# The gate and up products of two FFNs as seven half-size block products instead of eight

## The chip, the cores and the metric

The kernel runs on one core of one Trainium2 chip. The metric is the time of one execution on the device in microseconds; a kernel is run several times, and the median counts. The engines have the profile's names: PE is TensorE, which multiplies matrices (PEld its weight loads), DVE is VectorE, ACT ScalarE, POOL GpSimd, and SP's queue issues the DMA transfers.

## The reference

One decoder layer over T = 512 tokens with D = 1024 and FF = 2816, in float32:

```python
def swiglu(x, w_gate, w_up, w_down):
    return (jax.nn.silu(x @ w_gate) * (x @ w_up)) @ w_down
...
x = layer_norm(ALPHA * x + 0.5 * swiglu(x, ffn1_w_gate[l], ffn1_w_up[l], ffn1_w_down[l]), ln1_g[l], ln1_b[l])
proj = x @ w_in[l]
...
mix = jnp.concatenate([o_a, o_b], axis=-1) @ w_out[l]
x = layer_norm(ALPHA * x + mix, ln2_g[l], ln2_b[l])
x = layer_norm(ALPHA * x + 0.5 * swiglu(x, ffn2_w_gate[l], ffn2_w_up[l], ffn2_w_down[l]), ln3_g[l], ln3_b[l])
```

Between the two FFNs, `o_a` is a gated linear recurrence with four heads and `o_b` a depthwise convolution; this part is called the mixer here.

## The kernel before, in words

**Exact products in f32r.** Every operand of a large product is split into a high part (a cast to f32r on ScalarE) and a low part (the value less its high part, on VectorE): `split`, L59 to L61. `mm3` (L99 to L102) multiplies high by high, high by low and low by high into the same PSUM bank, so one product of 128x128 by 128x512 costs three matmuls.

**Weights.** They come in units of 128x1024 values. `fetch` (L64) issues the DMA on SP's queue, casts (`whi`, L60) and subtracts (`wlo`, L61). Six units' parts fit on chip (`SLOTS`), raw units have two buffers, and `ahead` keeps four units ready beyond the one in use.

**An FFN** (`ffn`, L243). The transposed activations x lie on chip as `xh`, `xl`. For each of 22 column blocks f of 128 columns there is a gate unit and an up unit: eight k of `mm3` each, 24 matmuls of 512 columns (the tokens). Then `evacuate` (L250 to L253): silu of the gate's bank on ScalarE, the product with the up bank on VectorE, and the cast and subtraction that make `hh`, `hl`, the parts of h. The first two column blocks are done differently: in FFN1 with the first four units and x arriving in growing pieces (L279 to L295), in FFN2 by `four_halved` (below).

**The down phase** is `rows_out` (L160): two halves of 512 output columns, 11 units each, four token tiles in four banks. The last four units of the second half go token tile by token tile. As each tile is done, VectorE adds it to the residual (L177) and takes statistics (L178, L182), GpSimd takes the root, VectorE scales (L186, L190), and TensorE transposes the normed tile (L134), whose parts ScalarE and VectorE make (L138). PE's order there is written by hand: tile 2's transposes, filler matmuls, tile 3's transposes and the rest of the filler. The filler, `four_halved` (L230), is the next phase's first four units over 256 columns, the first two token tiles before the others; before FFN2 these are its first two column blocks.

Outside the hand-written stretches a scheduler sets each engine's order when the program is built; on the chip an engine takes its instructions strictly in that order.

Of the kernel before, what the change touches and what calls it, by code (L numbers as in the profile page):

```python
# [16 lines left out]
P = 128  # L17
T = 512
# [4 lines left out]
NF = FF // P  # L23
NH = 4
# [21 lines left out]
def decoder_layer(ctx, tc, x_tok, x_t, vec, bcast, ng, w_gu1, w_d1, w_i, w_g, w_col, w_o, w_gu2, w_d2, out):  # L46
# [17 lines left out]
    def fetch(src, shape, lo_engine):  # L64
        raw = raws.tile([P, 1024], F32, tag="raw", name="raw")
        hi = parts.tile([P, 1024], F32R, tag="whi", name="whi")
        lo = parts.tile([P, 1024], F32R, tag="wlo", name="wlo")
        nc.sync.dma_start(out=raw, in_=src)
        split(raw, hi, lo, lo_engine)
        a, b = shape  # L70
        return hi.rearrange("p (a b) -> p a b", a=a), lo.rearrange("p (a b) -> p a b", a=a)

    todo, ready = deque(), deque()

    def ahead(n):
        while todo and len(ready) < n:
            ready.append(fetch(*todo.popleft()))

    def plan(srcs, shape, lo_engine):
        todo.extend((s, shape, lo_engine) for s in srcs)  # L80

    def unit():
        ahead(1 + AHEAD)
        return ready.popleft()

    tok, ch = (2, 512), (NK, P)
    plan([w_gu1[f, s] for f in range(2, NF) for s in range(2)], ch, nc.vector)
    plan([w_d1[h, u] for h in range(2) for u in range(NF // 2)], tok, nc.vector)
# [16 lines left out]
    xh = act.tile([P, NK, T], F32R, name="xh")  # L105
    xl = act.tile([P, NK, T], F32R, name="xl")
# [8 lines left out]
    gain = const.tile([P, D], F32, name="gain")  # L115
    bias = const.tile([P, D], F32, name="bias")

    def load_gb(i):
        nc.sync.dma_start(out=gain, in_=bcast[2 * i:2 * i + 1, :].broadcast_to([P, D]))
        nc.sync.dma_start(out=bias, in_=bcast[2 * i + 1:2 * i + 2, :].broadcast_to([P, D]))  # L120
# [18 lines left out]

    def scaled(i):  # L140
# [7 lines left out]
    def weave(main, fill):  # L148
        """main's steps, and as much of fill after each as its pause takes."""
# [10 lines left out]
    def rows_out(ks, per, lhs, accs, factor, late, finish, follow=()):  # L160
# [19 lines left out]
        def norm(i):  # L180
            mv = small.tile([P, 2], F32, tag="mv", name="mv")
# [12 lines left out]
        for u in range(n_units):  # L194
            hi, lo = unit()
            for i in range(NT):
                part(acc, u, hi, lo, i)
# [3 lines left out]
        for u in range(n_units - late):  # L201
            hi, lo = unit()
            for i in range(NT):
                part(acc, u, hi, lo, i)
        ahead(late)
        kept = [(u, *unit_now()) for u in range(n_units - late, n_units)]
        ahead(SLOTS - late)
        with tc.manual_schedule(engines={PE}):
            left = deque()
            for i in range(NT):  # L210
# [4 lines left out]
                if i == NT - 1:  # L215
# [11 lines left out]
    def unit_now():  # L227
        return ready.popleft()

    def four_halved(pp, banks):  # L230
        """Four units' columns, the first two token tiles before the others."""
        ahead(4)
        us = [unit_now() for _ in range(4)]
        pp.extend(bank(b) for b in banks)
# [8 lines left out]
    def ffn(first, meanwhile, finish, follow=()):  # L243
        with tc.tile_pool(name="ffn", bufs=1) as fp, tc.tile_pool(name="ffn2", bufs=2) as fp2:
            hh = fp.tile([P, NF, T], F32R, name="hh")
            hl = fp.tile([P, NF, T], F32R, name="hl")

            def evacuate(f, pg, pu):
                s = fp2.tile([P, T], F32, tag="s", name="s")
                nc.scalar.activation(s, pg, AF.Silu)  # L250
                nc.vector.tensor_tensor(s, pu, s, op=ALU.mult)  # L251
                nc.scalar.copy(hh[:, f, :], s)  # L252
                nc.vector.tensor_tensor(hl[:, f, :], s, hh[:, f, :].bitcast(F32), op=ALU.subtract)  # L253

# [18 lines left out]
    with tc.tile_pool(name="first", bufs=1) as fst:  # L273
        # the activation table loads while nothing else is there
# [4 lines left out]
        # the first four units and x come in interleaved, in growing pieces  # L279
        us = [(fst.tile([P, NK, P], F32, tag=f"raw{i}", name="raw"),  # L280
               *(parts.tile([P, 1024], F32R, tag=t, name=t).rearrange("p (a b) -> p a b", a=NK) for t in ("whi", "wlo")))
              for i in range(4)]
        for ks in (slice(0, 1), slice(1, 2), slice(2, 4), slice(4, 8)):
            x_raw = fst.tile([P, ks.stop - ks.start, T], F32, tag=f"xr{ks.start}", name="xr")
# [392 lines left out]
```

## Time and profile before

| | us |
|---|---|
| median of 3 runs | 977.93 (976.66 to 978.47) |
| profiled execution, span | 976.3 |
| TensorE busy, 4608 matmuls | 957.7 |
| its weight loads | 804.2 |
| VectorE busy | 472.1 |
| ScalarE busy | 276.0 |

Busy time is the sum over the span of what an engine's instructions took; matmuls overlap, so their recorded durations are longer than the distance from one start to the next. Where a cost is read below, it is read from starts. An operation over 128 partitions and 1024 elements in each is called 1024 wide.

### The profile page before, as it was taken

To read this page: it belongs to the slowest core of one execution; us is meant where nothing else is said; L and a number is where in the kernel's file an instruction comes from. 1 tells how busy PE (TensorE), PEld (TensorE's weight loads), DVE (VectorE), ACT (ScalarE), POOL (GpSimd) and SP (SyncE) were. 2 spreads that over 40 slices of the span, in tenths; PEclk is the share of its full clock that TensorE was granted. 3 is DMA by queue.
4 is the path that set the end of the run, shared out by engine and by line. 5 is a ranking of instruction groups with operands and counts; after the bars stand their busy time and mean duration, and the time that the engine had idled before them with its cause. 6 is when DMAs were issued, how large, how long until landed. Compare 5 with 4: busy or idle time off the path is not lost.

```text
span 976.3 us, 11214 instructions
## 1 busy us (share of the span) xinstructions
PE 957.7 (98%) x4608; PEld 804.2 (82%) x4608; DVE 472.1 (48%) x610; ACT 276.0 (28%) x376; POOL 119.9 (12%) x107
## 2 busy tenths in 40 slices
PE   7999999999999999999999999999999999999996
PEld 6888888888888889887888888988888888888885
DVE  6533333333224265999897658533333333322417
ACT  5423232323121213213331722432222223221200
POOL 8100000000000026522352203000000000000002
PEclk9999999999999999999999999999999999999998
DMA  7732323232222214311130121422222232323202
GB/s 265 247 116 87 108 87 106 88 105 90 98 97 96 98 44 141 130 65 50 59 127 4 65 93 43 172 103 90 105 88 107 87 107 87 108 87 109 87 21 87
DMA packets 28676, 96.49 MB, mean 99 GB/s; under 512 B 3200, under 2 KB 4736, under 8 KB 28496
## 3 DMA queue, kind: packets, MB, share of 16 engines
q1 hardware_dynamic: 28512, 95.43, 28.1%
q8 instruction: 36, 0.59, 0.2%
q0 software_dynamic: 112, 0.34, 0.2%
q14 instruction: 16, 0.13, 0.0%
HBM read 93.66 MB, written 2.10 MB: 98 GB/s over the span
## 4 chain that ended last, share of the span: by engine, by line
PE 81%; DVE 10%; issue 4%; POOL 2%; ACT 1%; DMA 1%; POOLq 0%; DVEq 0%; ACTq 0%
PE bank L101 26%; PE bank L102 26%; PE bank L100 26%; DVE bank L444 4%; PE bank L461 2%; DVE qk L493 1%; DVE xres L190 1%; POOL rstd L125 1%; DVE fq L411 1%; DVE diag L501 1%; POOL wlo L61 0%; DMA raw<-w_gu 0%; DVE tot L497 0%; DVE xl L138 0%; DMA raw<-w_g 0%
## 5 line engine op out<-in xcount | busy, mean ns | idle before, releaser
L100 PE MATMUL bank<-xh,whi 128*128 128x512 f32 (+1 forms) x896 | 336.9, 377 | 5.3 <-ACT whi L60 5.3
L101 PE MATMUL bank<-xl,whi 128*128 128x512 f32 (+1 forms) x896 | 335.8, 375 | 0.5 <-DVE xl L138 0.5
L102 PE MATMUL bank<-xh,wlo 128*128 128x512 f32 (+1 forms) x896 | 335.8, 375 | 0.0
L60 ACT CAST whi<-raw 128x1024 fp32r<-128x1024 f32 (+3 forms) x176 | 174.3, 995 | 560.2 <-PE bank L101 348.4
L61 DVE TENSOR_TENSOR wlo<-raw,whi 128x1024 fp32r<-128x1024 f32 (+3 forms) x154 | 176.8, 1155 | 301.1 <-ACT whi L60 297.1
L100 PEld LDWEIGHTS bank<-xh,whi 128*128 128x128 f32 x896 | 169.5, 189 | 35.7 <-ACT whi L60 5.8
L101 PEld LDWEIGHTS bank<-xl,whi 128*128 128x128 f32 x896 | 169.3, 189 | 30.7 <-DVE xl L138 0.8
L102 PEld LDWEIGHTS bank<-xh,wlo 128*128 128x128 f32 x896 | 169.3, 189 | 30.0
L100 PE MATMUL bank<-whi,hh 128*128 128x512 f32 x352 | 137.2, 390 | 0.0
L102 PE MATMUL bank<-whi,hl 128*128 128x512 f32 x352 | 137.0, 389 | 0.0
L101 PE MATMUL bank<-wlo,hh 128*128 128x512 f32 x352 | 137.0, 389 | 0.0
L124 POOL TENSOR_SCALAR rstd<-mv 128x1 f32<-128x1 f32 x16 | 8.1, 506 | 724.1 <-DVE mv L182 708.9
L251 DVE TENSOR_TENSOR s<-bank,s 128x512 f32<-128x512 f32 x44 | 30.3, 691 | 135.0 <-PE bank L102 134.3
L444 DVE SCALAR_TENSOR_TENSOR bank<-u,vecs,bank 128x512 f32<-128x512 f32 x120 | 82.0, 746 | 0.2
L102 PEld LDWEIGHTS bank<-whi,hl 128*128 128x128 f32 x352 | 66.1, 188 | 13.7
L100 PEld LDWEIGHTS bank<-whi,hh 128*128 128x128 f32 x352 | 66.1, 188 | 13.7
L101 PEld LDWEIGHTS bank<-wlo,hh 128*128 128x128 f32 x352 | 66.1, 188 | 13.5
L61 POOL TENSOR_TENSOR wlo<-raw,whi 128x1024 fp32r<-128x1024 f32 x22 | 53.0, 2414 | 78.3 <-ACT whi L60 78.2
L461 PEld LDWEIGHTS bank<-qk 128*128 128x128 f32 x256 | 30.6, 192 | 5.5 <-DVE qk L493 2.9
L461 PE MATMUL bank<-qk 128*128 128x128 f32 x256 | 31.8, 277 | 2.2 <-DVE qk L493 1.2
L253 DVE TENSOR_TENSOR hl<-s,hh 128x512 fp32r<-128x512 f32 x44 | 30.9, 703 | 0.0
L252 ACT CAST hh<-s 128x512 fp32r<-128x512 f32 x44 | 27.2, 622 | 0.0
(114 smaller groups left out, 601.5 us busy)
## 6 DMA issues: line engine op xcount, KB each, us to landing
raw<-w_gu SPq DMA_DIRECT2D x84, 512.0 KB, 3.2
raw<-w_d SPq DMA_DIRECT2D x44, 512.0 KB, 3.2
raw<-w_col SPq DMA_DIRECT2D x16, 512.0 KB, 3.2
raw<-w_o SPq DMA_DIRECT2D x8, 512.0 KB, 3.2
xres<-x_tok SPq DMA_DIRECT2D x4, 512.0 KB, 7.2
raw<-w_i SPq DMA_DIRECT2D x4, 512.0 KB, 3.1
raw<-w_g SPq DMA_DIRECT2D x4, 512.0 KB, 3.3
out<-xres SPq DMA_DIRECT2D x8, 256.0 KB, 2.0
```

What stands on the lines that cost most here:

```text
L60: nc.scalar.copy(hi, raw)
L61: lo_engine.tensor_tensor(lo, raw, hi.bitcast(F32), op=ALU.subtract)
L100: nc.tensor.matmul(ps, lhsT=lh, rhs=rh, start=first, stop=False)
L101: nc.tensor.matmul(ps, lhsT=lh, rhs=rl, start=False, stop=False)
L102: nc.tensor.matmul(ps, lhsT=ll, rhs=rh, start=False, stop=last)
L125: nc.gpsimd.tensor_tensor(r, r, negh.broadcast_to([P, n]) if n > 1 else negh, op=ALU.pow)
L190: nc.vector.scalar_tensor_tensor(xres[i][:, s], xres[i][:, s], r, bias[:, s], op0=ALU.mult, op1=ALU.add)
L251: nc.vector.tensor_tensor(s, pu, s, op=ALU.mult)
L252: nc.scalar.copy(hh[:, f, :], s)
L253: nc.vector.tensor_tensor(hl[:, f, :], s, hh[:, f, :].bitcast(F32), op=ALU.subtract)
L444: nc.vector.scalar_tensor_tensor(accs[n], us[n][:, j:j + T], vecs[:, w:w + 1], accs[n], op0=ALU.mult, op1=ALU.add)
L461: nc.tensor.matmul(ps[:, g, :], lhsT=k[:, h, sl], rhs=q[:, h, sl], start=True, stop=True)
```

## The change

**Seven products.** The tokens, the 1024 rows of a weight and the 2816 columns of a weight are each cut in half. A column block f of the first half of the columns goes together with block f + 11, so that there are 11 pairs of 2x2 block products. A gate block, and likewise an up block, is one `Quad`: a DMA of 1 MB with four 512-wide quarters b11, b12, b22, b21. With sums s1 to s4 of quarters of x and t1 to t4 of quarters of the weights, seven products p1 to p7 replace eight. Each is 4 k of three matmuls over 256 columns (half the tokens): 84 matmuls a block, where two units had 48 of 512 columns.

**The sums.** The x sums are made once per FFN (`Halves.sums`, four 1024-wide operations and the split of each). The weight sums are made for each block (`Quad.inner`): t1,t3 in one 1024-wide subtraction, t4 and t2 in two 512-wide ones. Every sum is split like a plain operand.

**The results.** A block has two PSUM banks, a and b. p2 is added onto p1, p4 onto p7 and p3 onto p5, each after ScalarE has copied the earlier one to SBUF (`Pair.steps`, L417); VectorE forms the sums (L419 to L422, L428). Silu and product are in `gate_up` (L473 to L477).

**h in f32.** h is no longer split at once but kept in f32, and the down phase's first half splits column pair u + 1 ahead of unit u (`before`, `parts_of`), into memory that held x and the early h. The gain and bias of each FFN's norm are loaded there too.

**The starts.** In FFN1, x comes in quarters and the first gate and up blocks in pieces; both p1 and both p2 go first (`EARLY`), the other products in the order of `LATER`. Before FFN2 the filler is these same four products (`begin`) and no longer four units; token tile 3's transposes are followed by `Halves.sums`.

```diff
@@ weights
+        def inner(self):
+            raw = self.raw
+            t13 = raws.tile([P, 2, 512], F32, tag="t13", name="t13", bufs=1)
+            nc.vector.tensor_tensor(t13, raw[:, 1:3, :], raw[:, 0:2, :], op=ALU.subtract)
+            self.both(("t1", "t3"), t13)
...
+            split(raw[:, 2:3, :], hi, lo, nc.vector)
+            self.name(("b22",), hi, lo)
+            nc.vector.tensor_tensor(raw[:, 1, :], raw[:, 2, :], t13[:, 0, :], op=ALU.subtract)
+            nc.vector.tensor_tensor(raw[:, 0, :], raw[:, 3, :], raw[:, 1, :], op=ALU.subtract)
+            self.both(("t4", "t2"), raw[:, 0:2, :])
@@ operand x
+        def sums(self):
+            (r11, r12), (r21, r22) = ([self.quarter(t, k) for k in range(2)] for t in range(2))
+            nc.vector.tensor_tensor(r22, r21, r22, op=ALU.add)
+            nc.vector.tensor_tensor(r21, r11, r21, op=ALU.subtract)
+            self.part("s3", r21)
+            self.part("s1", r22)
+            nc.vector.tensor_tensor(r11, r22, r11, op=ALU.subtract)
+            self.part("s2", r11)
+            nc.vector.tensor_tensor(r12, r12, r11, op=ALU.subtract)
+            self.part("s4", r12)
@@ products
+    SEVEN = {"p1": ("a11", "b11"), "p2": ("a12", "b21"), "p3": ("s4", "b22"), "p4": ("a22", "t4"),
+             "p5": ("s1", "t1"), "p6": ("s2", "t2"), "p7": ("s3", "t3")}
+    def product(ps, x, w, n, first=True):
+        xn, wn = SEVEN[n]
+        (xh, xl), (wh, wl) = x.of[xn], w[wn]
+        for k in range(4):
+            for j, (l, r) in enumerate(((wh, xh), (wh, xl), (wl, xh))):
+                nc.tensor.matmul(ps, lhsT=l[:, k, :], rhs=r[:, k, :], start=first and k == 0 and j == 0,
+                                 stop=k == 3 and j == 2, skip_group_check=True)
...
+                ps = {"p1": a[:, 0], "p2": a[:, 0], "p6": a[:, 1],
+                      "p7": b[:, 0], "p4": b[:, 0], "p5": b[:, 1], "p3": b[:, 1]}[n]
+                yield from product(ps, x, w, n, n in ("p1", "p5", "p6", "p7"))
+                if n in ("p1", "p7", "p5"):
+                    nc.scalar.copy(work[:, {"p1": 0, "p7": 1, "p5": 2}[n]], ps)
+                    if n == "p5":
+                        nc.vector.tensor_tensor(work[:, 1], work[:, 1], work[:, 2], op=ALU.add)
+                elif n == "p6":
+                    nc.vector.tensor_tensor(work[:, 0], a[:, 1], work[:, 0], op=ALU.add)
+                    nc.vector.tensor_tensor(work[:, 3], work[:, 0], work[:, 1], op=ALU.add)
...
+    EARLY, LATER = ("p1", "p2"), (("p7",), ("p4",), ("p5",), ("p6", "p3"))
+    USUAL = ("p1", "p7", "p2", "p4", "p5", "p6", "p3")
@@ ffn
-            for f in range(2, NF):
-                pp = []
-                for s in range(2):
-                    hi, lo = unit()
-                    ps = bank(2 * (f % 4) + s)
-                    for k in range(NK):
-                        mm3(ps, hi[:, k, :], lo[:, k, :], xh[:, k, :], xl[:, k, :], k == 0, k == NK - 1)
-                    pp.append(ps)
-                evacuate(f, *pp)
+                for f in range(1, NP):
+                    h.append(h_of(f))
+                    for s in range(2):
+                        ahead(3)
+                        w = unit_now()
+                        ahead(3)
+                        pr = Pair(pair_banks[f % 2][s], work_tile() if s else h[f])
+                        run(pr.steps(x, w, USUAL))
+                        gate_up(s, pr)
```

Three places show what this does to the engines' order.

VectorE, FFN1's start, before: behind the last piece of x come the last pieces of the first four units, and then the units after them.

```order
L61 TENSOR_TENSOR xl_74<-xr_153,xh_73 128x2048
L61 TENSOR_TENSOR wlo_95<-raw_93,whi_94 128x512
L61 TENSOR_TENSOR wlo_98<-raw_96,whi_97 128x512
L61 TENSOR_TENSOR wlo_101<-raw_99,whi_100 128x512
L61 TENSOR_TENSOR wlo_104<-raw_102,whi_103 128x512
L61 TENSOR_TENSOR wlo_271<-raw_269,whi_270 128x1024
L61 TENSOR_TENSOR wlo_277<-raw_275,whi_276 128x1024
```

The same place after the change; `xr_87` and `xr_88` are the raw quarters of x, `bl_86` holds the low parts of s1, s3 and s2 in this order, `raw_95` and `raw_96` are the first gate and up blocks, `t13_153` and `wlo_156` are the up block's t1,t3. Four operations stand between this piece and the split of a22 (`al_84`) ahead of it.

```order
L241 TENSOR_TENSOR xr_88<-xr_88 128x1024
L68 TENSOR_TENSOR wlo_128<-t13_125,whi_127 128x1024
L127 TENSOR_TENSOR raw_95<-raw_95 128x512
L242 TENSOR_TENSOR xr_88<-xr_87,xr_88 128x1024
L68 TENSOR_TENSOR bl_86<-xr_88,bh_85 128x1024
L68 TENSOR_TENSOR wlo_138<-raw_95,whi_137 128x1024
L68 TENSOR_TENSOR bl_86<-xr_88,bh_85 128x1024
L245 TENSOR_TENSOR xr_87<-xr_88,xr_87 128x1024
L120 TENSOR_TENSOR t13_153<-raw_96 128x1024
L247 TENSOR_TENSOR xr_87<-xr_87 128x1024
L68 TENSOR_TENSOR bl_86<-xr_87,bh_85 128x1024
L68 TENSOR_TENSOR wlo_156<-t13_153,whi_155 128x1024
```

The sums of x and both blocks' sums are now in one queue; the split of s3, which the first p7 needs, is the seventh row, and the last row is that of the up block's t3.

ScalarE, in the middle of FFN1's gate and up stage, before: each unit's cast, a silu, and the cast of h.

```order
L60 CAST whi_560<-raw_559 128x1024
L250 ACTIVATE s_554<-bank0_498 128x512
L60 CAST whi_591<-raw_590 128x1024
L252 CAST hh_324<-s_554 128x512
L60 CAST whi_627<-raw_626 128x1024
```

After the change, one gate block (`h_672` is its work tile, `bank4` its a, `bank6` its b) and the start of the up block (`work_1047`). The casts are those of a later block, `whi_1033` that of its t1,t3; the copies from `bank6` are those of p7 and p5.

```order
L417 COPY h_672<-bank4_930 128x256
L417 COPY h_672<-bank6_931 128x256
L65 CAST whi_1027<-raw_1025 128x1024
L65 CAST whi_1033<-t13_1031 128x1024
L417 COPY h_672<-bank6_931 128x256
L65 CAST whi_1043<-raw_1025 128x1024
L65 CAST w2hi_1037<-raw_1025 128x512
L417 COPY work_1047<-bank5_1048 128x256
L473 ACTIVATE h_672<-bank4_930 128x256
L474 ACTIVATE h_672<-h_672 128x768
L417 COPY work_1047<-bank7_1049 128x256
```

The cast of t1,t3 now stands ahead of the copy of p5, and the silu ahead of the up block's copy of p7.

VectorE, before FFN2, before the change: the last scaling of token tile 3 (`xres3_78`), the low parts of its transposes, and then units.

```order
L61 TENSOR_TENSOR wlo_4370<-raw_4368,whi_4369 128x1024
L190 SCALAR_TENSOR_TENSOR xres3_78<-xres3_78,rstd_4378,bias_86 128x512 x2
L138 TENSOR_TENSOR xl_74<-bank6_4479,xh_73 128x4x128
L138 TENSOR_TENSOR xl_74<-bank7_4486,xh_73 128x4x128
L61 TENSOR_TENSOR wlo_4613<-raw_4611,whi_4612 128x1024
L251 TENSOR_TENSOR s_4634<-bank1_4386,s_4634 128x512
```

After the change, from the same scaling on; `xr_5298` and `xr_5299` are raw quarters of x, `bl_5297` the low parts of s1 and s3, `raw_5301` and `raw_5625` weight blocks.

```order
L335 SCALAR_TENSOR_TENSOR xres3_76<-xres3_76,rstd_5481,m1_3845 128x512 x2
L68 TENSOR_TENSOR wlo_5612<-t13_5609,whi_5611 128x1024
L126 TENSOR_TENSOR raw_5301<-raw_5301,t13_5609 128x512
L278 TENSOR_TENSOR al_5295<-bank7_5565,ah_5294 128x4x128
L127 TENSOR_TENSOR raw_5301<-raw_5301 128x512
L120 TENSOR_TENSOR t13_5631<-raw_5625 128x1024
L241 TENSOR_TENSOR xr_5299<-xr_5299 128x1024
L68 TENSOR_TENSOR wlo_5622<-raw_5301,whi_5621 128x1024
L242 TENSOR_TENSOR xr_5299<-xr_5298,xr_5299 128x1024
L68 TENSOR_TENSOR bl_5297<-xr_5299,bh_5296 128x1024
L245 TENSOR_TENSOR xr_5298<-xr_5299,xr_5298 128x1024
L68 TENSOR_TENSOR bl_5297<-xr_5299,bh_5296 128x1024
```

Between the last transposes' low parts and the split of s3 now stand the sums of x and pieces of two weight blocks.

## Rows read from the trace of the kernel before

**Rows 1.** The page, part 1: engine, busy time, share of the span, instructions.
```profile
PE 957.7 (98%) x4608; PEld 804.2 (82%) x4608; DVE 472.1 (48%) x610; ACT 276.0 (28%) x376; POOL 119.9 (12%) x107
```

**Rows 2.** The page, part 4: the chain that ended last, shares of the span.
```profile
PE 81%; DVE 10%; issue 4%; POOL 2%; ACT 1%; DMA 1%; POOLq 0%; DVEq 0%; ACTq 0%
```

**Rows 3.** Windows: stretch, us; busy (count) of PE, PEld, DVE, ACT, POOL; PEclk, DMA, GB/s.
```profile
100.00:125.00 25.00, 25.00 (x112) 20.72 (x111) 8.71 (x9) 7.92 (x10) 0.00 (x0) 1.00 0.26 88
375.00:400.00 25.00, 25.00 (x191) 24.08 (x190) 14.85 (x22) 9.67 (x11) 16.52 (x9) 1.00 0.46 167
...
970.00:972.00 2.00, 0.00 (x0) 0.00 (x0) 1.56 (x3) 0.00 (x0) 1.68 (x2) 0.57 0.00 0
```

**Rows 4.** Timeline of VectorE, gate and up stage: start, duration, engine, line, operation, idle before.
```profile
106.53 0.69 DVE L251 TENSOR_TENSOR s<-bank,s 128x512 f32<-128x512 f32 x1 [3.42 <-PE bank L102]
...
117.41 0.69 DVE L251 TENSOR_TENSOR s<-bank,s 128x512 f32<-128x512 f32 x1 [3.42 <-PE bank L102]
```

**Rows 5.** Timeline of TensorE, 256-column fillers after FFN1's down phase.
```profile
374.77 0.28 PE L100 MATMUL bank<-xh,whi 128*128 128x256 f32 x1
...
379.69 0.28 PE L102 MATMUL bank<-xh,wlo 128*128 128x256 f32 x1
```

**Rows 6.** Timeline of TensorE: FFN1's first matmuls, and where each FFN's third column block begins.
```profile
6.71 0.63 PE L101 MATMUL bank<-xl,whi 128*128 128x512 f32 x1
7.13 0.63 PE L102 MATMUL bank<-xh,wlo 128*128 128x512 f32 x1
...
10.97 0.70 PE L100 MATMUL bank<-xh,whi 128*128 128x512 f32 x2
...
30.10 0.39 PE L100 MATMUL bank<-xh,whi 128*128 128x512 f32 x1
...
630.74 0.40 PE L100 MATMUL bank<-xh,whi 128*128 128x512 f32 x1
```

**Rows 7.** Timeline of VectorE: 1024-wide splits at the start, 512-wide ones before FFN2.
```profile
11.70 1.23 DVE L61 TENSOR_TENSOR xl<-xr,xh 128x1024 fp32r<-128x1024 f32 x1 [1.67 <-ACT xh L60]
12.84 1.95 DVE L61 TENSOR_TENSOR wlo<-raw,whi 128x256 fp32r<-128x256 f32 x4
...
604.33 1.27 DVE L138 TENSOR_TENSOR xl<-bank,xh 128x512 fp32r<-128x512 f32 x2
605.52 2.34 DVE L61 TENSOR_TENSOR wlo<-raw,whi 128x1024 fp32r<-128x1024 f32 x2
```

**Rows 8.** Timeline of ScalarE, at the start and in the gate and up stage.
```profile
5.66 0.21 ACT L307 ACTIVATE e<-e 128x8 f32<-128x8 f32 x1 [1.13 <-DVE e L306]
...
11.57 1.02 ACT L60 CAST whi<-raw 128x256 fp32r<-128x256 f32 x3
...
122.56 1.05 ACT L60 CAST whi<-raw 128x1024 fp32r<-128x1024 f32 x1 [3.80 <-PE bank L101]
123.51 0.59 ACT L250 ACTIVATE s<-bank 128x512 f32<-128x512 f32 x1
```

**Rows 9.** Timeline of both engines where a filler matmul waits for VectorE.
```profile
369.25 1.27 DVE L138 TENSOR_TENSOR xl<-bank,xh 128x512 fp32r<-128x512 f32 x2
...
369.98 0.38 PE L101 MATMUL bank<-xl,whi 128*128 128x256 f32 x1 [0.52 <-DVE xl L138]
370.20 0.28 PE L102 MATMUL bank<-xh,wlo 128*128 128x256 f32 x1
```

**Rows 10.** Timeline around the start of FFN2: VectorE's norms, TensorE's fillers and transposes.
```profile
599.17 0.67 DVE L177 SCALAR_TENSOR_TENSOR xres<-bank,xres 128x512 f32<-128x512 f32 x1
...
604.97 0.28 PE L100 MATMUL bank<-xh,whi 128*128 128x256 f32 x1
...
614.69 1.41 DVE L190 SCALAR_TENSOR_TENSOR xres<-xres,rstd,bias 128x512 f32<-128x512 f32 x2
...
615.58 1.29 PE L134 MATMUL bank<-ident,xres 128*128 128x128 f32 x8 [0.54 <-DVE xres L190]
```

**Rows 11.** The page, part 6: DMA issues, KB each, us to landing.
```profile
raw<-w_gu SPq DMA_DIRECT2D x84, 512.0 KB, 3.2
```

More of the change, by code (lines that the diff above doesn't have):

```diff
@@ L82, in unit, with plan_quads, plan_two, unit_now @@
+    def plan(srcs, shape, lo_engine):
+        todo.extend(("unit", s, shape, lo_engine) for s in srcs)
+    def plan_quads(srcs):
+        todo.extend(("quad", s) for s in srcs)
+    def plan_two(srcs):
+        todo.append(("two", *srcs))
+    def unit_now():
+        return ready.popleft()[1]
     def unit():
         ahead(1 + AHEAD)
-        return ready.popleft()
+        return unit_now()
     tok, ch = (2, 512), (NK, P)
-    plan([w_gu1[f, s] for f in range(2, NF) for s in range(2)], ch, nc.vector)
@@ L114, in decoder_layer, with load_gb @@
     masks = const.tile([P, len(MASKED) + 1, P], U8, name="masks")
[L115 to L120, printed above, removed]
+    gb = []
+    def load_gb(i, t):
+        gb[:] = [t[:, 0, :], t[:, 1, :]]
+        for j in range(2):
+            nc.sync.dma_start(out=t[:, j, :], in_=bcast[2 * i + j:2 * i + j + 1, :].broadcast_to([P, D]))
     def rstd_of(square, scale, eps, n):
@@ L158, in weave, with rows_out @@
                 owed -= t
-    def rows_out(ks, per, lhs, accs, factor, late, finish, follow=()):
+    def rows_out(ks, per, lhs, accs, factor, late, finish, follow=(), before=lambda u: None, then=lambda: None,
+                 fill=True):
         n_units = len(ks) // per
@@ L180, in norm @@
         def norm(i):
+            gain, bias = gb
             mv = small.tile([P, 2], F32, tag="mv", name="mv")
@@ L214, in rows_out @@
                         left.popleft()()
[L215 removed]
+                if i == NT - 1 and fill:
                     ahead(SLOTS)
@@ new lines, in decoder_layer, with work_tile, begin, early @@
+    EARLY, LATER = ("p1", "p2"), (("p7",), ("p4",), ("p5",), ("p6", "p3"))
+    USUAL = ("p1", "p7", "p2", "p4", "p5", "p6", "p3")
+    def work_tile():
+        return small.tile([P, 4, H], F32, tag="work", name="work", bufs=2)
+    def begin(begun, x, pair_banks):
+        ahead(2)
+        w2 = [unit_now() for _ in range(2)]
+        pairs = [Pair(pair_banks[0][s], work_tile()) for s in range(2)]
+        begun.extend((w2, pairs))
+        return early(x, w2, pairs)
+    def early(x, w2, pairs):
+        for n in EARLY:
+            for w, pr in zip(w2, pairs):
+                yield from pr.steps(x, w, (n,))
@@ L277, in decoder_layer, with load_x @@
         nc.scalar.activation(one, one, AF.Exp)
[L280 to L284, printed above, removed]
-            nc.sync.dma_start(out=x_raw, in_=x_t[:, ks, :])
-            for i, (raw, hi, lo) in enumerate(us):
-                nc.sync.dma_start(out=raw[:, ks, :],
-                                  in_=w_gu1[i // 2, i % 2, :, ks.start * P:ks.stop * P].rearrange("p (a b) -> p a b", b=P))
-            split(x_raw, xh[:, ks, :], xl[:, ks, :], nc.vector)
-            for raw, hi, lo in us:
-                split(raw[:, ks, :], hi[:, ks, :], lo[:, ks, :], nc.vector)
-        first = [bank(i) for i in range(4)]
-        for k in range(NK):
-            for ps, (_, hi, lo) in zip(first, us):
-                mm3(ps, hi[:, k, :], lo[:, k, :], xh[:, k, :], xl[:, k, :], k == 0, k == NK - 1)
-        ahead(2)
+        def load_x(t, k):
+            nc.sync.dma_start(out=x1.quarter(t, k), in_=x_q[t, k])
+        qs = [Quad(w_gu1[0, s]) for s in range(2)]
+        steps = [q.outer(True) for q in qs]
+        load_x(0, 0)
+        for q in qs:
+            q.load(0, 1)
+        load_x(0, 1)
+        for q in qs:
+            q.load(3, 4)
+        for k in range(2):
+            load_x(1, k)
+        for q in qs:
+            q.load(1, 3)
+        for k in range(2):
+            x1.part(f"a1{k + 1}", x1.quarter(0, k))
+            for st in steps:
+                st(k)
+        x1.part("a22", x1.quarter(1, 1))
+        qs[0].inner()
+        x1.sums()
+        qs[1].inner()
+        w2 = [q.of for q in qs]
+        pairs = [Pair(BANKS1[0][0][s], work_tile()) for s in range(2)]
+        with tc.manual_schedule(engines={PE}):
+            run(early(x1, w2, pairs))
         make_identity(nc, ident)
```

284 lines of the change are left out of this document (222 added, 62 removed).

## The prediction

> **What bounds the kernel now.** I read the page's busy shares first [rows 1]: TensorE is busy 98% of the 976.3 us, VectorE 48%, ScalarE 28%. The chain that ended last agrees [rows 2]: 81% TensorE, and only 4% in which an engine waited for nothing the profile shows. So time comes off by giving TensorE less to do, and goes on wherever TensorE is made to wait. The windows [rows 3] tell which stage has room: in the gate and up stage (100 to 125 us) TensorE is busy 25.00 of 25, VectorE 8.71, ScalarE 7.92. In 375 to 400, where matmuls are 256 columns wide, TensorE's own weight loads fill 24.08 of 25.
>
> The pitch comes from two timelines. VectorE multiplies a column block in at 106.53 and the next at 117.41 [rows 4]: 10.88 us for 48 matmuls of 512 columns, 0.2267 us each. The 256-column fillers start at 374.77 and, 41 matmuls later, at 379.69 [rows 5]: 0.120 us each. Two narrow ones cost 6% more than a wide one.
>
> **The steady blocks: −32.0.** One old unit pair (two units, 48 wide matmuls) is 10.88 us. One new block does the same work in 84 narrow ones, 84 × 0.120 = 10.08. Leaving out the first gate and up blocks of each FFN, that is 20 blocks a time: 20 × 0.80 = 16.0 for each FFN. The seven-for-eight saving alone would be 12.5%; the narrow pitch leaves 7.4%. The Trainium skill (TensorE: Matmul & The Clock Gate, section Back-to-back issue gap) lists 518 cycles for 512 columns and 262 for 256, so it would charge 1% for halving, not 6%; by it 48 wide ones less 84 narrow ones are 2856 cycles, 1.19 us at 2.4 GHz, a block, the term −47.6 and the time 965.9 (an estimate from that page). The trace does not agree, with 0.120 beside 0.2267; its rows are of this kernel's own f32r stream, and I use them.
>
> **VectorE under the steady blocks: nothing, narrowly.** Starts give the prices [rows 7]: a 1024-wide operation 12.84 − 11.70 = 1.14 us, a 512-wide one 0.60 (two in 605.52 − 604.33). A column block pair (a gate and an up block) needs eight 1024-wide, eight 512-wide, seven 256-wide and one 768-wide operation; with 0.34 and 0.87 estimated between and below those prices, 17.2 us of the 20.16 that TensorE takes. By the durations instead of the starts it is about 19.3. It fits if nothing stalls it; what it would cost without that cover is the second rival. ScalarE has four 1024-wide casts at 0.95 [rows 8] and smaller copies, 9.7 of 20.16. A block's 1 MB must come every 10 us where 0.5 MB came every 5.4 and landed in 3.2 us [rows 11]: hidden behind the blocks fetched ahead. In the down phase one more split of h (1.14 us) stands in each 5.4 us unit beside the unit's own 1.14: nothing, and the mixer's instructions stay. The gain and bias rows of each FFN's norm are now fetched on SP's queue between the units of the down phase's first half: nothing, since a transfer of that size (128x1024) lands in about 3.2 us [rows 11] and the norm is a half phase away.
>
> **Waits inside a block: +8.0.** Product p3 accumulates where p5 lay, so it waits for ScalarE's copy of p5. In ScalarE's order the cast of the next t1,t3 stands ahead of that copy, and it can only start when p5, the last reader of the old t1, is done. Behind the waiting p3 stand the next block's products, and VectorE's last sum waits for it. After p5: 0.08 us, cast 0.95, copy 0.38 (a 256-wide cast takes 0.31 [rows 8], a PSUM read a little more) = 1.41; then 0.05 to be seen (the first operation of the pair at 369.25 is done about 369.92, the matmul starts at 369.98 [rows 9]) and 0.10 for a matmul that waited (369.98 to 370.20 is 0.22 instead of 0.12) = 1.56 against the 1.44 of p6 that should cover it: 0.12 lost. In an up block the copy of p7 stands behind the silu, which waits for VectorE's last sum: about 0.05 more in half of the blocks. 40 blocks: 5.8, and about 1.1 in the first block of each FFN: 8.0. Bounds: 0, where the copy is in time by 0.1 us, and 16, where cast and copy each take 0.2 longer.
>
> **FFN1's start: +16.4.** Before, the first two column blocks are done at 30.10 [rows 6]. Now the operand sums go through VectorE first. ScalarE's first cast is queued behind the exponential at 5.66 [rows 8], so VectorE begins about 6.9 and is through the first six splits (two wide, four of 512: 4.7) at 11.6. Its next row needs the cast of a22, which ScalarE has queued behind the copies of both p1; these run at the slow pitch of 0.427 for 512 columns [rows 6], 0.22 for 256, and end at 13.2; copies and cast (0.95) take it to 14.8. From that row to the split of s3 (the second bl_86 in the order shown) stand eight wide operations and three of 512, 10.9: 25.7, and the first p7 runs then. The five behind, to the split of the up block's t1,t3 (wlo_156), take 5.7: 31.4. TensorE, done with the early p1 and p2 about 16, waits nearly all that time. It returns slow: p7 2.3 and a p4 2.6, and seven products at 1.44: 46.5. Bounds 43 (the queue not held at 14.8 but run through from 6.9: wlo_156 done at 28.2) to 48 (every product at the slow pitch up to 38).
>
> **FFN2's start: +11.1.** The old filler of four whole units ran from 604.97 until the wide products began at 630.74 [rows 6, 10], covering norm and transposes of the last tile. The new filler is p1 and p2 of two blocks, 48 matmuls, 5.8 us: with transposes between, TensorE is out of work at 611.6. From VectorE's add at 599.17 [rows 10] its new order up to the last norm is 15.0 us: 614.2 (before, that norm's second half starts at 614.69 and the transposes at 615.58, behind other splits). Transposes to 615.1, and then the sums: from the norm to the split of s3, eight wide and three of 512, 10.9 us: 625.1. TensorE idles about 10 us. The two p7 cost 5.1 at the slow pitch, eight products 11.5: 641.8. Bounds +9 (no slow clock) and +13.5.
>
> That the clock goes while idle is in the windows: after the last matmul at about 968 the granted clock of 970 to 972 is 0.57 of full [rows 3], and at the start the pitch stays slow until 10.97 [rows 6].
>
> **Sum.** −32.0 + 16.4 + 11.1 + 8.0 = +3.5 on the profiled 976.3: 979.8. The median of the runs is 977.93, 1.6 above the span: **981.5**.
>
> **The rivals.**
> *The copies come in time* (the other side). If the copy of p5 gets in within p6's 1.44 us, the waits cost 1 and not 8: 974.5, faster by 0.35%. The place is ScalarE between p5 and p3, the point 0.12 us: the waits must cost less than 2.5 in all to end below 976. For it: 0.12 is within what cast and copy can vary; against it: the order puts the cast first in every block.
> *VectorE becomes the bound.* If splits wait for casts that wait for VectorE's own subtractions, a pair takes not 20.16 but, say, its 19.3 and 3 us of waits, 22.3: 20 pairs × 2.15 = 43, in place of the 8 above: 1016. For it: the margin is 0.9 us by durations; against it: parts are ready two to four ahead.
> *Weight loads pace the narrow matmuls.* A load's share in 375 to 400 is 24.08 us over 190 loads, 0.127 each, but if they did not overlap with each other, at the 0.19 that the old stage shows (20.72 over 111 [rows 3]), a block would take 84 × 0.19 = 15.8 us: 40 × 5.7 = +228, about 1210. The pitch of 0.120 held for 41 matmuls [rows 5] speaks against it. The Trainium skill (same title, same section) says that in a stream of load and matmul pairs the spacing is set by both; the trace agrees only in so far as two narrow matmuls cost more than one wide.
> *The narrow pitch is half of the wide one.* 0.1134 × 84 = 9.52, another 0.55 off 40 blocks: 959.5. Rows 5 speak against it; the mechanism would be that the wide ones, not the narrow ones, carry no extra. The Trainium skill's table of cycles (TensorE: Matmul & The Clock Gate, Back-to-back issue gap) comes nearest to this; the trace does not agree, with 0.120 against 0.1134.
>
> That the block does not compute in seven can be left out: its order has 84 matmuls a block.
>
> **How the numbers follow.** About 0.2% is what a measurement of this kernel can tell from no change: 976.0 to 979.9 counts as the same. The forecast has 0.58 (its own range 976 to 990 from the bounds above), the copies in time 0.27, VectorE's bound 0.11, the loads 0.02, the half pitch 0.02. Faster: 0.25 of the second, 0.02 of the last, 0.02 of the forecast's low end (both starts at their lower bounds give −3.4 − 2.1): 0.29. Same: 0.02 of the copies, 0.13 of the forecast: 0.15. Slower: 0.56. The range of 8 in 10 is 966 (copies in time, both starts at the lower bounds, 969, and a little of the half pitch) to 997 (the forecast's upper bounds: 981.5 + 8 + 2.4 + 1.5, and the low part of VectorE's case).
>
> **What would show it.** Right: TensorE idle between about 16 and 31 and between 612 and 625, with a granted clock near half in both; the first column blocks done at 46.5 and 641.8; 84 matmuls per block at 0.120; VectorE busy about 85% of the gate and up stage; and waits of some 0.1 us of TensorE on ScalarE's copies, once per block. Wrong: a pitch other than 0.120; waits on VectorE's low parts in the middle of the stage (the second rival); no wait at p3 (the first); or starts done before 43 and 640.

## The result and the profile after

The changed kernel takes 988.9 us (median of 4 runs, 987.96 to 989.03), the kernel before 978.08 (4 runs): 1.011 times as long, 95% interval 1.0095 to 1.0124. Slower by 10.8 us, where 981.5, slower by 3.6, was forecast. The profiled execution is the fastest of the four; its span is 986.1 us, 9.8 more than the span before.

The page's busy times and chain [rows 1, 2]:

```profile
PE 934.5 (95%) x6096; PEld 855.0 (87%) x6096; DVE 743.2 (75%) x987; ACT 397.8 (40%) x577; POOL 120.4 (12%) x107
...
PE 74%; DVE 15%; issue 4%; POOL 2%; DMA 2%; ACT 2%; POOLq 0%; DVEq 0%; ACTq 0%
```

TensorE is busy 23 us less than before and the span is 10 us longer: of its span it now stands idle some 52 us, where it was 19. VectorE has gone from 48% to 75%, and its share of the chain from 10% to 15%. Where TensorE waits, the view of its waits says (who waited for whom: us in total, times, longest):

```profile
PE bank L397 <- ACT bh L65: 18.9, 2, 10.8
PE bank L397 <- ACT whi L65: 10.9, 2, 9.5
PE bank L397 <- DVE bl L68: 3.5, 2, 1.8
PE bank L259 <- DVE xres L335: 2.0, 1, 2.0
...
PE bank L397 <- ACT work L417: 0.4, 1, 0.4
```

The rows for `bh` and `bl` are two places, one in each FFN's start; most of the `whi` row (9.5) is the wait for the first operands of all. The windows around the starts and of the steady stage (columns as in [rows 3]):

```profile
19.00:29.00 10.00, 0.00 (x0) 0.00 (x0) 10.00 (x8) 3.63 (x4) 7.47 (x5) 0.66 0.02 7
29.00:32.00 3.00, 0.65 (x2) 0.36 (x2) 3.00 (x4) 0.55 (x1) 0.00 (x0) 0.50 0.19 22
100.00:200.00 100.00, 100.00 (x828) 99.44 (x827) 87.35 (x119) 51.92 (x79) 0.00 (x0) 1.00 0.29 102
626.00:635.00 9.00, 0.89 (x7) 0.49 (x5) 9.00 (x11) 6.69 (x8) 1.78 (x1) 0.71 0.15 35
```

From 19 to 29 TensorE does nothing at all and VectorE is busy 10.00 of 10; from 626 to 635 TensorE is busy 0.89 of 9. The granted clock is 0.66 and 0.71 of full in these two windows, and 0.50 from 29 to 32. In the steady stage TensorE is busy 100.00 of 100, its loads 99.44, VectorE 87.35. The boundaries between the stages, first matmuls of: the second pair of blocks, FFN1's down phase, the filler before FFN2, FFN2's second pair, its down phase:

```profile
52.94 0.28 PE L397 MATMUL bank<-ah,whi 128*128 128x256 f32 x1
...
257.31 0.40 PE L188 MATMUL bank<-whi,hh 128*128 128x512 f32 x1
...
616.28 0.28 PE L397 MATMUL bank<-ah,whi 128*128 128x256 f32 x1
...
654.36 0.28 PE L397 MATMUL bank<-ah,whi 128*128 128x256 f32 x1
...
857.88 0.40 PE L188 MATMUL bank<-whi,hh 128*128 128x512 f32 x1
```

The two down phases of before began at:

```profile
247.70 0.39 PE L100 MATMUL bank<-whi,hh 128*128 128x512 f32 x1
...
848.37 0.39 PE L100 MATMUL bank<-whi,hh 128*128 128x512 f32 x1
```

With the other boundaries of before (30.10 and 630.74 [rows 6], 604.97 [rows 10]) these give the whole difference of the spans:

| stretch | forecast | measured |
|---|---|---|
| FFN1 to the second pair | +17.5 | 52.94 − 30.10 = +22.8 |
| FFN1's 20 steady blocks | −13.1 | 204.37 − 217.60 = −13.2 |
| down phase, mixer, to the filler | 0 | 358.97 − 357.27 = +1.7 |
| FFN2, filler to the second pair | +12.2 | 38.08 − 25.77 = +12.3 |
| FFN2's 20 steady blocks | −13.1 | 203.52 − 217.63 = −14.1 |
| FFN2's down phase and the end | 0 | 128.22 − 127.93 = +0.3 |
| sum | +3.5 | +9.8 |

(Forecast: the 8.0 of waits shared out, 2.9 to each 20 blocks and 1.1 to each start.) Two rows are off against the forecast: FFN1's start by 5.3, and 1.7 in front of the mixer. FFN2's steady blocks save 1.0 more than forecast.

### The profile page after: what moved, and what is told of

The parts are those of the page before. It is cut to its first block, busy times and chain, and to the rows that moved or that the text cites. A ratio compares the mean times of both kernels' runs of the same rounds, so it can differ in the third digit from the quotient of the medians.

```text
span 986.1 us, 14697 instructions
## 1 busy us (share of the span) xinstructions
PE 934.5 (95%) x6096; PEld 855.0 (87%) x6096; DVE 743.2 (75%) x987; ACT 397.8 (40%) x577; POOL 120.4 (12%) x107
## 4 chain that ended last, share of the span: by engine, by line
PE 74%; DVE 15%; issue 4%; POOL 2%; DMA 2%; ACT 2%; POOLq 0%; DVEq 0%; ACTq 0%
PE bank L397 44%; PE bank L190 9%; PE bank L189 9%; PE bank L188 9%; DVE bank L729 4%; PE bank L746 2%; DVE xres L335 2%; DVE wlo L68 1%; POOL wlo L68 1%; DMA raw<-w_col 1%; DMA vecs<-vec 1%; DVE bl L68 1%; DVE m L778 1%; POOL rstd L216 1%; DVE diag L786 1%
## 5 line engine op out<-in xcount | busy, mean ns | idle before, releaser
L68 DVE TENSOR_TENSOR wlo<-raw,whi 128x1024 fp32r<-128x1024 f32 (+1 forms) x144 | 174.0, 1213 | 146.4 <-ACT whi L65 146.2
L65 ACT CAST whi<-raw 128x1024 fp32r<-128x1024 f32 (+1 forms) x166 | 172.3, 1041 | 259.7 <-PE bank L190 140.7
L397 PE MATMUL bank<-bh,whi 128*128 128x256 f32 x528 | 152.0, 288 | 20.3 <-ACT bh L65 18.9
L397 PE MATMUL bank<-ah,whi 128*128 128x256 f32 x528 | 151.6, 287 | 9.8 <-ACT whi L65 9.5
L397 PE MATMUL bank<-bl,whi 128*128 128x256 f32 x528 | 151.9, 288 | 3.5 <-DVE bl L68 3.5
L397 PE MATMUL bank<-al,whi 128*128 128x256 f32 x528 | 151.3, 287 | 1.0 <-DVE al L278 0.8
L397 PE MATMUL bank<-bh,wlo 128*128 128x256 f32 x528 | 151.5, 287 | 0.8 <-DVE wlo L68 0.8
L397 PE MATMUL bank<-ah,wlo 128*128 128x256 f32 x528 | 151.2, 286 | 0.3 <-DVE wlo L68 0.3
L188 PE MATMUL bank<-whi,hp 128*128 128x512 f32 x320 | 124.7, 390 | 0.0
L190 PE MATMUL bank<-whi,hp 128*128 128x512 f32 x320 | 124.5, 389 | 0.0
L189 PE MATMUL bank<-wlo,hp 128*128 128x512 f32 x320 | 124.5, 389 | 0.0
```

The source lines that it names most:

```text
L188: nc.tensor.matmul(ps, lhsT=lh, rhs=rh, start=first, stop=False)
L189: nc.tensor.matmul(ps, lhsT=lh, rhs=rl, start=False, stop=False)
L190: nc.tensor.matmul(ps, lhsT=ll, rhs=rh, start=False, stop=last)
L397: nc.tensor.matmul(ps, lhsT=l[:, k, :], rhs=r[:, k, :], start=first and k == 0 and j == 0, stop=k == 3 and j == 2, skip_group_check=True)
```

## The experiments

Each is the changed kernel with one edit unless it says otherwise; times are medians of four runs or more, beside the kernel before on the same chip (977.6 to 978.1). In e1, e3 and e4 part of some sums is lost, where a product begins anew in one half of a bank before the other half has all its parts (e5 and e10 avoid this and lose none); the number of matmuls is unaffected. In e2 and e9 FFN1's residual is not scaled.

### What makes p3 late in a steady block

The wait that was forecast for each block stands in the trace. ScalarE and TensorE in one block (start, duration):

```profile
101.16 1.05 ACT L65 CAST whi<-t 128x1024 fp32r<-128x1024 f32 x1 [1.83 <-PE bank L397]
102.11 0.37 ACT L417 COPY h<-bank 128x256 f32<-128x256 f32 x1
...
102.40 0.28 PE L397 MATMUL bank<-bh,wlo 128*128 128x256 f32 x1
102.53 0.38 PE L397 MATMUL bank<-ah,w2hi 128*128 128x256 f32 x1
102.76 0.28 PE L397 MATMUL bank<-al,w2hi 128*128 128x256 f32 x1
```

p5 ends; ScalarE casts the next t1,t3 (101.16), then copies p5 (102.11 to 102.48), and p3 starts at 102.53, 0.13 behind the last of p6 (102.40) and 0.23 ahead of its own next matmul instead of 0.12. A block takes 10.17 us, not 10.08. The step is at p3 in all 40 blocks; the view of waits lists none of them. (The 0.4 above is a p2 in FFN1's last up block, at 249.91: the copy of p1 stood behind the silu there.) e1 and e5 give the copy of p5 more cover.

```diff
-    USUAL = ("p1", "p7", "p2", "p4", "p5", "p6", "p3")
+    USUAL = ("p1", "p7", "p5", "p2", "p4", "p6", "p3")
```

> Edit: in the steady blocks p5 is moved to the third place (p1, p7, p5, p2, p4, p6, p3), so that its copy has three products of 1.44 us as cover. Theory A (p3 waits for the copy of p5, which stands behind the cast of the next t1,t3): the 0.23 us step at p3's first matmul goes, a block takes 10.08 instead of 10.17 us, the 20 blocks of an FFN 201.6 instead of 204.4 and 203.5; time about 984.5. Theory B (the step belongs to p3's own operands, b22 in a tile of its own): the step stays at p3, a block stays at 10.17, time 988 to 990.

Measured: 1031.2 us. The 0.23 step at p3 is gone, but a larger wait has come:

```profile
PE bank L397 <- ACT work L417: 20.8, 18, 1.6
PE bank L397 <- ACT h L417: 9.3, 20, 0.5
```

Nearly every p5 now waits for the copy of p7 just ahead of it, which reads the other half of the same bank, and in up blocks this copy stands behind the silu (up to 1.6 us). These two rows hold 30.1 of the 42.3 us that e1 is slower than the change. Neither theory had that: the step at p3 went as A said, the time did not.

```diff
-    USUAL = ("p1", "p7", "p2", "p4", "p5", "p6", "p3")
+    USUAL = ("p7", "p1", "p4", "p5", "p2", "p6", "p3")
```

> Edit: the steady blocks' products in the order p7, p1, p4, p5, p2, p6, p3: p5's copy has two products (2.9 us) as cover, p5 starts in bank b when p7 and p4 are done there, so that the results are those of the change. Theory A (p3's step is the late copy of p5): a block takes 10.08 us instead of 10.17, the 20 blocks 201.6; time 984 to 985.5. Theory B (the copies are late wherever they stand, behind ScalarE's casts and silu): the wait moves to p4, whose copy of p7 has only p1 (1.44 us) as cover; blocks of 10.15 or more, time 988 or more.

Measured: 987.2 us, 1.7 less than the change, and between the times of A and B. TensorE around p3:

```profile
71.35 0.28 PE L397 MATMUL bank<-bh,wlo 128*128 128x256 f32 x1
71.47 0.28 PE L397 MATMUL bank<-ah,w2hi 128*128 128x256 f32 x1
...
81.55 0.28 PE L397 MATMUL bank<-ah,w2hi 128*128 128x256 f32 x1
```

p3 starts 0.12 behind p6, the next block's p3 10.08 later: the step is gone, as A said. Of the 2.8 and 1.9 us that were to be had, part comes back as three waits at p4 (B's place) where the silu is late, in the last up block of each FFN and one near FFN2's start:

```profile
PE bank L397 <- ACT work L417: 3.0, 3, 1.2
```

In this trace another 1.5 us is lost in front of the mixer (its section, last paragraph), so the step shows more than the time does.

Is VectorE near its limit, as the second rival had it? e8 adds an operation per block:

```diff
             split(value, hi, lo, nc.vector)
+            if names[0] == "b11":
+                rest(lo, value, hi)
```

> Edit: in each block VectorE makes the low parts of b11,b21 twice (one more 1024-wide operation of 1.14 us a block, 2.28 a pair). Theory A (VectorE has 2.5 us of 20.35 to spare in a pair, as 87.35 of 100 us busy say): the blocks stay at 10.17 us, time 988 to 992. Theory B (VectorE is at its limit already): each pair gets about 2 us longer, time 1020 to 1035.

Measured: 988.2 us, no longer than the change. Window of the steady stage:

```profile
100.00:200.00 100.00, 100.00 (x834) 99.94 (x834) 99.17 (x132) 51.42 (x81) 0.00 (x0) 1.00 0.30 106
```

VectorE takes 99.17 us of 100 and TensorE still does not wait for it: the cover of 2.5 us a pair was real. The run also has an answer on p3 that it was not made for. The added work shifted the engines' order, and in 16 of FFN1's 20 steady blocks ScalarE's copy of p5 now stands ahead of the cast of t1,t3 (181.44 and 181.70 in one of them): these have no step at p3, and 834 matmuls fit into the window instead of 828. Where the cast still comes first (191.35, copy at 192.30), p3 starts late (192.72, its next matmul 0.22 later). So the unchanged time is not the price of the added operation alone. The third rival's price is gone as well: a load does not take 0.19 us, since a matmul with its load starts every 0.12. Whether the loads, busy 99.94 of 100, are what sets that 0.12 is not shown.

### FFN1's start: what was missed

VectorE and GpSimd in the change, VectorE's first split and then 20 to 28 us:

```profile
8.95 1.22 DVE L68 TENSOR_TENSOR al<-xr,ah 128x1024 fp32r<-128x1024 f32 x1
...
20.43 1.52 DVE L126 TENSOR_TENSOR raw<-raw,t 128x512 f32<-128x512 f32 x1
21.86 2.05 DVE L241 TENSOR_TENSOR xr<-xr 128x1024 f32<-128x1024 f32 x1
23.84 2.05 DVE L68 TENSOR_TENSOR wlo<-t,whi 128x1024 fp32r<-128x1024 f32 x1
25.82 1.52 DVE L127 TENSOR_TENSOR raw<-raw 128x512 f32<-128x512 f32 x1
27.26 1.21 DVE L242 TENSOR_TENSOR xr<-xr 128x1024 f32<-128x1024 f32 x1
...
20.04 6.75 POOL L284 TENSOR_SCALAR xres<-xres 128x1024 f32<-128x1024 f32 x4
```

A 1024-wide sum took 2.05 us (21.86) and the same form at 27.26, when GpSimd had finished, 1.21; one of 512 took 1.52 where 0.68 is usual. All the while GpSimd scaled the residual, four operations in 6.75 us. e2 leaves these out.

```diff
             nc.sync.dma_start(out=xres[i], in_=x_tok[i])
-            scaled(i)
```

> Edit: the four scalings of the residual by ALPHA, which GpSimd does between 20.0 and 26.8 us, are left out in FFN1 (so the residual is not scaled there). Theory A (GpSimd and VectorE slow each other when both run): VectorE's operations of 20.4 to 27 us, which took 1.52 and 2.05 us, take 0.69 and 1.21 as elsewhere; the split of the up block's t1,t3 ends at about 34.2 instead of 37.5, the first pair of blocks is done at 49.6 instead of 52.9; time about 985.5. Theory B (those VectorE operations are slow by themselves, as sums of two raw operands): they stay at 1.52 and 2.05 and the time stays at 988 to 990.

Measured: 985.2 us, −3.7. VectorE in the same place:

```profile
20.49 0.68 DVE L126 TENSOR_TENSOR raw<-raw,t 128x512 f32<-128x512 f32 x1
21.09 1.21 DVE L241 TENSOR_TENSOR xr<-xr 128x1024 f32<-128x1024 f32 x1
22.22 1.21 DVE L68 TENSOR_TENSOR wlo<-t,whi 128x1024 fp32r<-128x1024 f32 x1
23.36 0.68 DVE L127 TENSOR_TENSOR raw<-raw 128x512 f32<-128x512 f32 x1
```

The four slow operations are back at 0.68 and 1.21, and the first pair is done at 49.64, 3.30 earlier: theory A. The Trainium skill has the rule (SBUF — State Buffer, section Who interferes with whom): a VectorE instruction with two inputs in SBUF contends with a GpSimd instruction that reads SBUF. The trace agrees, with 0.84 us more on each of the four.

The other part is the beginning. ScalarE in the change, then in e6, where the small vectors (`vecs`, for the lower bounds) are fetched behind x and the weights:

```profile
7.77 0.21 ACT L582 ACTIVATE e<-e 128x8 f32<-128x8 f32 x1 [5.49 <-DVE e L581]
7.89 1.03 ACT L65 CAST ah<-xr 128x1024 fp32r<-128x1024 f32 x1
```

```profile
4.93 1.04 ACT L65 CAST ah<-xr 128x1024 fp32r<-128x1024 f32 x1 [2.65 <-DMA xr<-x_q]
```

```diff
-        nc.gpsimd.dma_start(out=vecs, in_=vec)
...
     def load_rest():
+        nc.sync.dma_start(out=vecs, in_=vec)
+        l0, l1 = vecs[:, V_LB:V_LB + NH], vecs[:, V_LB + NH:V_LB + 2 * NH]
...
```

> Edit: the packed vectors and the lower bounds made of them come behind x and the first weights, so that ScalarE's first cast does not stand behind the exponential at 7.77 us. Theory A (that wait set the start of VectorE's queue): first cast at 6.3 to 7.0 instead of 7.89, the first pair done 1 to 1.5 us earlier (51.5 to 52), time 987.4 to 988. Theory B (x and the weights land no earlier than that): first cast still after 7.6, time within 0.5 of the change's 988.9.

Measured: 986.3 us (ratio to before 1.0077, interval 1.005 to 1.0104; four runs spread from 981.1 to 987.2). The first cast moves from 7.89 to 4.93 and the pair is done at 50.38, 2.56 earlier: theory A, by twice what it said. The forecast had put the exponential at 5.66, where it stood before [rows 8]; but its vectors land 5.9 us after they are asked for, not 3.3, and the cast waits behind it. That they land later because x now comes in larger pieces beside them is likely, but no run shows it. Both edits together:

> Edit: e2 and e6 together in the change (FFN1's residual not scaled, the lower bounds behind x). Theory A (what the prediction missed at FFN1's start is GpSimd's scalings, 3.3 us, and the late first cast, 2.5): the first pair is done at about 47.1 instead of 52.9, 46.5 having been forecast, and the time is 982.5 to 983.5. Theory B (one hides the other, since the queue waits elsewhere): the pair is done at 49 or later, time 985 or more.

Measured: 983.2 us. The second pair begins at:

```profile
46.73 0.28 PE L397 MATMUL bank<-ah,whi 128*128 128x256 f32 x1
```

46.73, where 46.5 and 1.1 of waits were forecast. The missed 5.3 us are these two, and they add: 3.30 and 2.56 alone, 6.21 together. That is 0.9 more than was missed: without them the rest of the forecast for this start is 0.9 too long.

### In front of the mixer

VectorE's last two scalings of FFN1's norm, GpSimd beside them, and the transposes that wait:

```profile
385.76 5.67 DVE L335 SCALAR_TENSOR_TENSOR xres<-xres,rstd,gb 128x512 f32<-128x512 f32 x2
...
385.57 5.31 POOL L68 TENSOR_TENSOR wlo<-raw,whi 128x1024 fp32r<-128x1024 f32 x2 [0.69 <-ACT whi L65]
...
391.58 0.63 PE L259 MATMUL bank<-ident,xres 128*128 128x128 f32 x4 [2.02 <-DVE xres L335]
```

Two operations of 0.74 took 5.67 us (2.90 and 2.84), while GpSimd made the low parts of two units. GpSimd began 0.19 us ahead of them. Before, the same pair took 1.41, and GpSimd began 0.85 us behind its start:

```profile
376.62 1.41 DVE L190 SCALAR_TENSOR_TENSOR xres<-xres,rstd,bias 128x512 f32<-128x512 f32 x2
...
377.47 5.18 POOL L61 TENSOR_TENSOR wlo<-raw,whi 128x1024 fp32r<-128x1024 f32 x2 [1.72 <-ACT whi L60]
```

e7 gives these two units to VectorE.

```diff
-    plan([w_col[n] for n in (0, 4, 1, 5, 12, 13, 14, 15)], ch, nc.gpsimd)
+    plan([w_col[n] for n in (0, 4)], ch, nc.vector)
+    plan([w_col[n] for n in (1, 5, 12, 13, 14, 15)], ch, nc.gpsimd)
```

> Edit: the low parts of two units of the mixer, which GpSimd made between 385.6 and 390.9 us, are made by VectorE. Theory A (VectorE's two last scalings of FFN1's norm took 2.84 and 2.90 us instead of 0.74 because GpSimd ran a two-operand subtraction beside them): they take 0.7 to 0.75, TensorE's wait of 2.02 us at the last transposes goes or falls under 0.5, time 986.5 to 987.5. Theory B (their wait is for the root from GpSimd or for the bank): the scalings stay above 1.5 us and the wait stays.

Measured: 986.0 us, −2.9. The pair:

```profile
389.51 1.41 DVE L336 SCALAR_TENSOR_TENSOR xres<-xres,rstd,gb 128x512 f32<-128x512 f32 x2
```

1.41 us for both, and of the wait of 2.02 at the transposes 0.4 is left: theory A. The time, 0.5 below A's range, is another matter. Between the two traces the stretch from the down phase to the filler shrinks from 358.97 to 358.04, 0.93 of the 1.70, for the two units' low parts now stand on VectorE ahead of the pair, which ends at 390.92 instead of 391.43. Where the rest of the −2.9 comes from the traces do not show; their spans differ by 1.1.

The wait of 2.0 us has a second price, which comes and goes. The 4.2 us from the last transposes on, in the traces of e6 and of the change (columns as in [rows 3]):

```profile
388.46:392.66 4.20, 4.20 (x23) 4.20 (x24) 1.15 (x2) 0.59 (x1) 1.26 (x5) 0.59 0.40 125
391.58:395.78 4.20, 4.20 (x36) 4.20 (x37) 1.14 (x2) 0.59 (x1) 1.26 (x5) 1.00 0.37 129
```

TensorE had waited 2.03 and 2.02 us. In e6 the granted clock was 0.59 behind this and 23 matmuls ran, in the change 1.00 and 36. It was 0.59 in e5 and 0.63 in e4 as well, 1.00 in e2, e3 and e9. Where it fell, the stretch from the down phase to the filler is 360.5 to 360.9 us long, elsewhere 359.0. So 1.5 us or more of a time can hang on this place, whatever the edit was meant to do, and gains of that size (e5's, and part of e6's) rest on the rows shown and not on the time.

### The starts without sums

If the sums are what TensorE waits for, plain products for the first pair cost 24 more matmuls (2.9 us) and take the sums off the path. e3 does that in FFN2, e4 in both.

```diff
+        def plain(self):
+            self.both(("b12", "b22"), self.raw[:, 1:3, :])
...
+    PLAIN = (("a11", "b11", 0, 0, True), ("a12", "b21", 0, 0, False), ("a11", "b12", 0, 1, True), ("a12", "b22", 0, 1, False),
+             ("a21", "b11", 1, 0, True), ("a21", "b12", 1, 1, True), ("a22", "b21", 1, 0, False), ("a22", "b22", 1, 1, False))
...
-                for ns in LATER:
+                for ns in LATER if len(begun) == 2 else ():
```

> Edit: in FFN2 the first gate and up blocks are eight plain products (192 matmuls of 256 columns in all instead of 168), so the sums of x and of these weights are off the path; FFN1 as in the change. Theory A (the sums on VectorE's queue cost 12 us at this start): from the first filler matmul to the third column block 25.8 us as in the kernel before, not 38.1; the steady blocks stay as they are; time 977 to 979. Theory B (VectorE owes the same work either way): the first steady blocks wait instead, and the time falls by less than 4 us, 985 or more.

Measured: 977.8 us, the time of the kernel before (1.0001, interval 0.9991 to 1.001). The filler's first matmul and the second pair's:

```profile
616.44 0.28 PE L417 MATMUL bank<-ah,whi 128*128 128x256 f32 x1
...
642.95 0.28 PE L402 MATMUL bank<-ah,whi 128*128 128x256 f32 x1
```

26.5 us between them, 25.8 in the kernel before, 38.1 in the change: theory A. VectorE's debt is paid under the steady blocks; of B there is 1.2 us, since FFN2's 20 blocks take 204.7 and not 203.5.

> Edit: the first gate and up blocks of both FFNs are eight plain products. Theory A: FFN1's first pair is done at 34 to 37 us instead of 52.9 (192 matmuls at 0.12 from about 9.5, some at the slow pitch), FFN2's start as in e3; time 957 to 964, below the kernel before. Theory B (VectorE, with the sums and the first blocks' sums still to do, holds the next blocks up): FFN1's third pair of blocks starts less than 6 us earlier than in the change, time 970 or more.

Measured: 965.7 us, 0.9872 of the kernel before (0.9858 to 0.9887). FFN1's second pair, and a wait in it:

```profile
35.48 0.28 PE L402 MATMUL bank<-ah,whi 128*128 128x256 f32 x1
...
43.29 0.39 PE L402 MATMUL bank<-ah,whi 128*128 128x256 f32 x1 [3.16 <-ACT h L444]
```

The second pair starts at 35.48 instead of 52.94; 3.16 us of this go back at p2, whose copy of p1 is queued on ScalarE behind casts of sums that are still under way, and in this trace 1.9 in front of the mixer, where the clock fell. A, with that much of B; the time is 1.7 above the range of A.

> Edit: the first pairs of both FFNs as plain products (in FFN2 the half-bank products one after another, so that all results are those of the reference), with e6 and e7. Theory A (the gains of e4, e6 and e7 add up, being three separate waits): 965.7 less 2.5 and 2.5, 959.5 to 962. Theory B (with plain products the start is bound by TensorE, so that the earlier first cast does not add): 963 or more.

Measured: 961.8 us, 0.9839 (0.9824 to 0.9854): A, at its upper end.

> Edit: e10 with the order of products of e5. Theory A: the blocks take 10.08 instead of 10.17 us, 1.7 us or more off e10, 957 to 960. Theory B (p7 first asks for s3 and t3 one product earlier, when VectorE is still behind after the start): the first steady blocks wait and it is e10's time or more.

Measured: 957.9 us (956.25 to 961.1), 0.9803 of the kernel before, interval 0.9782 to 0.9824: theory A. Busy times, and the steady window:

```profile
PE 928.5 (97%) x6144; PEld 853.1 (89%) x6144; DVE 715.8 (75%) x956; ACT 387.7 (41%) x562; POOL 118.4 (12%) x104
...
100.00:200.00 100.00, 100.00 (x836) 100.00 (x835) 86.63 (x120) 51.30 (x80) 0.00 (x0) 1.00 0.31 106
```

It computes all that the kernel before does and is 2% faster than that and 3% faster than the change.

## Why the prediction was right and where it failed

**Sign and shape: right; the amount three times too small.** The steady blocks save what the 0.120 pitch allows less a wait of 0.1 per block, and the starts give back more. The pitch stood (blocks of 10.08 in e5). The sign does not rest on the misses below: without the 5.3 and the 1.7 the span would still be 2.8 longer. Of the median's 10.8 us, 1.0 is not in the spans.

**Waits inside a block: right in place and size.** 2.8 and 1.9 us against 2.9 for 20 blocks; the cast-then-copy sequence reads in the trace as it was added up, e5 takes it away, and e8 shows it coming and going with the order of cast and copy. The 0.05 for the copy of p7 in up blocks is not there: the steps are at p3 alone. The first rival (copies in time) is so refuted for the change and made true by e5.

**VectorE under the blocks: right.** 17.2 us of 20.16 were forecast, 87.35% of 20.35 is 17.8; e8 shows the margin. The second rival would have needed VectorE to stall. For ScalarE the forecast counted four 1024-wide casts a pair; the trace has six, and its 51.92% is 10.6 us of a pair instead of 9.7, without consequence.

**FFN2's start: right.** +12.3 against +12.2: the norm's end, eight wide and three narrow operations (626.01 to 637.21, 11.2 us where 10.9 was said), and the slow return are there, and with the sums off the path e3 leaves 0.7 of the 12.3.

**FFN1's start: mis-sized, +22.8 against +17.5.** Two steps failed. "ScalarE's first cast is queued behind the exponential at 5.66, so VectorE begins about 6.9": it began at 8.95, since the vectors landed later (e6: 2.6 us). And "eight wide operations and three of 512, 10.9" took its price of 1.14 from 11.70 us [rows 7], where GpSimd ran only small 128x128 operations; beside the scalings four operations of the chain took 0.84 longer each (e2: 3.3 us). The range named for this term, 43 to 48, left both out. The rule of the Trainium skill that is cited with e2 bears on this step, and the trace has its price.

**"The mixer's instructions stay": true of their order, not of their time.** Shifted by a us against each other, GpSimd's subtractions now began just ahead of VectorE's pair instead of within it, and the pair took 5.67 us instead of 1.41. The wait of 2.0 that this makes at the transposes covers the +1.7. e7 shows the cause of the slow pair, and gets back 0.93 of the 1.70.

## What to carry to other kernels

A scheme that trades matmuls for sums pays at every place where its operands are new: count the sums that stand ahead of the first product as a chain on their engine, and do the first block the plain way while they are made. Price each operation of that chain with what runs beside it there, not from a quiet stretch. A copy that lets an accumulator be reused must be queued ahead of anything that waits for the same product.

## What the runs showed of the hardware that was not expected

VectorE and GpSimd slow each other much more than their sizes suggest: a 512-wide VectorE operation of 0.74 us lasted 2.90 and 2.84 beside GpSimd's 1024-wide subtractions of 2.7, while beside GpSimd's scalings it was 0.84 more whatever its width (0.68 to 1.52, 1.21 to 2.05). And the way back to the full clock differed. After 11 us of idling in FFN1, TensorE ran at about half the clock from 29.6 to 43 us (0.51 from 31 to 43), with waits of 1.75, 1.41 and 0.76 us in its return; after 8 us in FFN2 from 634.9 to 643.4 (0.50 from 635 to 643), with one wait of 1.75. After the 2.0 us wait in front of the mixer the clock fell in some executions and not in others.
